# A two-layer decoder trunk: forget gates projected ahead of queries, norms by pairs and by log and exp, conditioning products ahead of the recurrence, weights two blocks ahead

## The chip, the cores and the metric

The kernel runs on one core of one Trainium2 chip. The metric is the device time of one execution in microseconds (us). The time before is 1189.71 us, the median of 3 runs (1188.65 to 1191.13). The profile is of one further execution.

## The reference, cut to what matters

A sequence of 256 tokens with 1024 features passes six sub-layers: feed-forward, recurrence (HGRN2), feed-forward, feed-forward, gated MLP, feed-forward. Each sub-layer has a norm before and behind it, and a shift, a scale and a gate that come from one vector `c`.

```python
mod = (silu(c) @ ada_w[i] + ada_b[i])            # shift, scale, gate of three sub-layers
def sublayer(x, fn, pre_g, post_g, shift, scale, gate, res_w):
    h = rms_norm(x, pre_g) * (1.0 + scale) + shift
    return x + res_w * gate * rms_norm(fn(h), post_g)

def hgrn2_mix(h, w_in, w_out, out_norm, lb):
    q, f, i, g = split(h @ w_in)                 # 1024 columns each, 8 heads of 128
    q = silu(q)
    log_f = logaddexp(log(lb), log1p(-lb) + log_sigmoid(f))
    k = (1.0 - lb) * sigmoid(-f)
    ...                                          # per head, chunks of 64: S_t = diag(f_t) S_{t-1} + k_t i_t^T
    o = rms_norm(o, out_norm) * silu(g)          # o_t = S_t^T q_t, norm per head
    return o @ w_out
```

## The kernel before, in words

**Weights.** Every weight block is 1 MB and comes in two halves (`cast`, `sub`): SyncE issues a load into one of four `raw` buffers (L121), ScalarE rounds the half to the high part (L122), VectorE subtracts to make the low part (L132). Products take three passes (high by high, high by low, low by high). The blocks stand in one list in the order of their use; `next_block` makes blocks until more than `ahead` are ready. High and low parts take buffers of a pool of 14. `proj`, `feat` and `tok` project with these blocks.

**Conditioning products.** The vector from `c` is made by 144 products on VectorE (`ada`, L192), each with a load of 512 KB into one of three buffers (after the first sub-layer has begun), issued by the same SyncE queue, in program order with the weights. `pace(upto, blocks)` spreads them: `wblock` makes both halves of a block, adds `rate` to a credit, and makes one product for each whole credit. `gate_tile` and `pre_cols` call for those that are still missing where they are used (products up to 24s+24 for the gate of sub-layer s, up to 24s+16 for its shift and scale).

**The recurrence sub-layer** (`hgrn`): two half projections of the output gate `g` and the values `v` stand in the sub-layer's entry (`boundary`, `proj`). Then come `feat` for the queries of heads 0 to 3, `feat` for their forget gates with `gate_f` (absolute value, exp and log on ScalarE, running sums on VectorE), and the recurrence `attn(0)`, stepped by `zip_steps` against `feat` for the queries and gates of heads 4 to 7 and `tok` for the other values. `attn` has a diagonal product (L718), then seven levels of 64, 32, ... 1 rows: VectorE prepares an operand (L741, L746), ScalarE takes the exponential (L80), VectorE multiplies (L752), TensorE makes the product (L758), VectorE merges it (L729); between two levels TensorE runs a part of the projections. Last come the outputs (L793). `attn(1)` runs beside `norm` (of the first four heads), `tok` for the rest of `g`, and `outs` (transposes L836, `split` L844 and L845, output products). Behind it stand the norm of the other heads (`stats`, `turn`) and the `boundary` to the next sub-layer.

**Order.** In `open()` to `close()` regions the instructions run as written; elsewhere a scheduler orders each engine's queue by program order and readiness. ScalarE, VectorE and TensorE take their queues in order, so an instruction that waits holds all behind it.

Of the kernel before, what the change touches and what calls it, by code (L numbers as in the profile page):

```python
# [18 lines left out]
P = 128  # L19
# [6 lines left out]
EPS = 1e-6  # L26
# [7 lines left out]
class Body:  # L34
# [272 lines left out]
    def boundary(self, y, G, mm, cols, table, plan=(4, 2, 0, 0)):  # L307
# [40 lines left out]
        gated(1, 0, yg1)  # L348
        self.alloc_h()
# [32 lines left out]
        dve = self.h_low(1, 1, self.h_full(1, pa1, cols))  # L382
        self.halves(1)
# [101 lines left out]
    def ffn(self, f, hT, G_fn, pre_next, nxt, bg):  # L485
# [100 lines left out]
        if f == 0:  # L586
            self.pace(bg, 23)
        for u in range(len(pend), 11):
# [17 lines left out]
            if u == 8:  # L606
                G = G_fn()
        pre_next()
# [35 lines left out]
    def hgrn(self, hT, G_fn, pre_next, nxt, bg):  # L644
        nc, tc = self.nc, self.tc
        self.pace(bg, 8)
# [152 lines left out]
        def stats(hb, ops, sqrt):  # L799

            ss = self.tiny.tile([P, 8], F32, tag="ss8", name="ss8")
            r = self.tiny.tile([P, 8], F32, tag="r8", name="r8")
            og, sqs = self.t4(), []
            for u in range(2):
                sqs.append(self.t2().rearrange("p (i v) -> p i v", i=4))
                nc.scalar.activation(sqs[u], ops[u].rearrange("p t h v -> p (t h) v"), AF.Square)

            def gated(u):
                c0 = 2 * (2 * hb + u) * P
                nc.vector.tensor_mul(og[:, 512 * u:512 * u + 512].rearrange("p (t c) -> p t c", t=NT),  # L810
                                     ops[u].rearrange("p t h v -> p t (h v)"), gg[:, :, c0:c0 + 2 * P])

            for u in range(2):
                nc.vector.reduce_sum(ss[:, 4 * u:4 * u + 4], sqs[u], axis=mybir.AxisListType.X)
                if u == 0:
                    gated(0)
            nc.vector.tensor_scalar(ss, ss, 1.0 / P, EPS, op0=ALU.mult, op1=ALU.add)
            if sqrt:
                self.tact(ss, ss, AF.Sqrt)
                self.cast()  # L820
                gated(1)
                nc.vector.reciprocal(r, ss)
            else:
                gated(1)
                self.rsqrt(r, ss)
            return og, r

        def turn(hb, u, og, r):

            on = og[:, 512 * u:512 * u + 512].rearrange("p (i v) -> p i v", i=4)  # L830
            for i in range(4):
                nc.vector.tensor_scalar(on[:, i, :], on[:, i, :], r[:, 4 * u + i:4 * u + i + 1], None, op0=ALU.mult)
# [89 lines left out]
        def norm():  # L922
            with tc.high_priority(offset=400):
                state["norm"] = stats(0, ops[0], False)
            yield

        def outs():
            for u in range(2):
                split(0, u, turn(0, u, *state["norm"]))
# [8 lines left out]
        y = []  # L938
        zip_steps(attn(1, bank_a, ops[1]), [
# [4 lines left out]
        self.table("sqrt_and_others")  # L944
        self.ahead = 0
        fill = products(1)
        wos = [nb()]
        self.ahead = 1
        wos.append(nb())
        self.open()  # L950
        self.gate = state["ops"]
        for op in fill[:5]:
            op()
# [5 lines left out]
        for op in fill[6:]:  # L959
            op()  # L960
        for u in range(2):
            split(1, u, ps[u])
# [338 lines left out]
```

## Time and profile before

| what | us |
|---|---|
| median of 3 runs | 1189.71 |
| profiled execution | 1182.1 |
| its span, first to last instruction | 1180.3 |
| TensorE busy | 1141.9 |
| VectorE busy | 904.6 |
| ScalarE busy | 665.9 |

Busy times are unions over an engine's instructions. Matmuls are pipelined, so TensorE's busy time says only where it stood still; how fast it went is read from the distance between the starts of two matmuls and from the granted clock (PEclk).

### The profile page before, as it was taken

To read this page: it belongs to the slowest core of one execution; us is meant where nothing else is said; L and a number is where in the kernel's file an instruction comes from. 1 tells how busy PE (TensorE), PEld (TensorE's weight loads), DVE (VectorE), ACT (ScalarE), POOL (GpSimd) and SP (SyncE) were. 2 spreads that over 40 slices of the span, in tenths; PEclk is the share of its full clock that TensorE was granted. 3 is DMA by queue.
4 is the path that set the end of the run, shared out by engine and by line. 5 is a ranking of instruction groups with operands and counts; after the bars stand their busy time and mean duration, and the time that the engine had idled before them with its cause. 6 is when DMAs were issued, how large, how long until landed. Compare 5 with 4: busy or idle time off the path is not lost.

```text
span 1180.3 us, 17103 instructions
## 1 busy us (share of the span) xinstructions
PE 1141.9 (97%) x6518; PEld 997.0 (84%) x6518; DVE 904.6 (77%) x1379; ACT 665.9 (56%) x1046; POOL 6.8 (1%) x16
## 2 busy tenths in 40 slices
PE   7999999997988999999999999999999999999997
PEld 6999998896877788888888888888989988888886
DVE  6997866899878799886599887466878776865752
ACT  6554436667636865556566555564665367654541
POOL 0000000000000000000000000000000000000000
PEclk9999999997989999999999999999999999999999
DMA  9889986597224399887279988526777773777630
GB/s 355 308 315 339 315 297 213 189 345 269 86 76 160 112 355 354 321 310 233 99 275 345 339 307 276 188 81 207 264 272 248 259 260 108 244 239 226 218 126 36
DMA packets 79765, 282.31 MB, mean 239 GB/s; under 512 B 9874, under 2 KB 10562, under 8 KB 79683
## 3 DMA queue, kind: packets, MB, share of 16 engines
q1 hardware_dynamic: 78626, 278.05, 67.4%
q0 software_dynamic: 1056, 3.17, 0.8%
q8 instruction: 51, 0.84, 0.3%
q14 instruction: 32, 0.25, 0.1%
HBM read 280.11 MB, written 1.07 MB: 238 GB/s over the span
## 4 chain that ended last, share of the span: by engine, by line
PE 77%; DVE 9%; DMA 8%; ACT 4%; issue 2%; SPq 0%; DVEq 0%; ACTq 0%
PE ups L454 17%; PE ups L455 9%; PE y L164 8%; PE y L162 8%; PE y L163 8%; PE pps L429 7%; PE ups L574 4%; DVE w L132 3%; DMA ada<-in_ada 3%; DMA raw<-in_wgmu 2%; PE ups L460 2%; PE ups L462 2%; PE ups L461 2%; PE ab L758 2%; ACT w L122 2%
## 5 line engine op out<-in xcount | busy, mean ns | idle before, releaser
L132 DVE TENSOR_TENSOR w<-raw,w 128x1024 fp32r<-128x1024 f32 x376 | 453.2, 1221 | 87.0 <-ACT w L122 85.4
L122 ACT CAST w<-raw 128x1024 fp32r<-128x1024 f32 x376 | 387.6, 1049 | 158.0 <-DMA raw<-in_wffn 75.3
L454 PE MATMUL ups<-h,w 128*128 128x512 f32 x864 | 302.1, 393 | 0.0
L455 PE MATMUL ups<-h,w 128*128 128x256 f32 x864 | 242.0, 280 | 0.0
L192 DVE CUSTOM_DVE_ANT_0 ada<-ada,cond 128x1024 f32<-128x1024 f32 x144 | 173.9, 1219 | 33.0 <-DMA ada<-in_ada 33.0
L454 PEld LDWEIGHTS ups<-h,w 128*128 128x128 f32 x864 | 161.7, 187 | 36.5
L162 PE MATMUL y<-w,t 128*128 128x512 f32 x448 | 178.6, 399 | 1.6 <-ACT t L167 1.6
L164 PE MATMUL y<-w,t 128*128 128x512 f32 x448 | 177.3, 396 | 0.4 <-DVE t L168 0.4
L163 PE MATMUL y<-w,t 128*128 128x512 f32 x448 | 177.3, 396 | 0.0
L455 PEld LDWEIGHTS ups<-h,w 128*128 128x128 f32 x864 | 163.3, 189 | 1.0
L460 PE MATMUL ups<-h,w 128*128 128x256 f32 x416 | 118.4, 285 | 0.0
L462 PE MATMUL ups<-h,w 128*128 128x256 f32 x416 | 117.7, 283 | 0.0
L461 PE MATMUL ups<-h,w 128*128 128x256 f32 x416 | 117.6, 283 | 0.0
L429 PE MATMUL pps<-w,h 128*128 128x512 f32 x480 | 113.9, 393 | 0.8 <-DVE be L242 0.8
L429 PEld LDWEIGHTS pps<-w,h 128*128 128x128 f32 x480 | 89.0, 188 | 19.4 <-DVE h L291 1.2
L162 PEld LDWEIGHTS y<-w,t 128*128 128x128 f32 x448 | 84.3, 188 | 21.5 <-ACT t L167 2.5
L164 PEld LDWEIGHTS y<-w,t 128*128 128x128 f32 x448 | 84.2, 188 | 21.4 <-DVE t L168 1.2
L163 PEld LDWEIGHTS y<-w,t 128*128 128x128 f32 x448 | 84.3, 188 | 18.2 <-DVE w L132 0.3
L460 PEld LDWEIGHTS ups<-h,w 128*128 128x128 f32 x416 | 79.7, 192 | 1.1 <-issue 0.2
L461 PEld LDWEIGHTS ups<-h,w 128*128 128x128 f32 x416 | 79.7, 192 | 0.8 <-issue 0.2
L462 PEld LDWEIGHTS ups<-h,w 128*128 128x128 f32 x416 | 79.7, 192 | 0.0
L80 ACT ACTIVATE t<-t 128x256 f32<-128x256 f32 (+2 forms) x70 | 36.1, 522 | 51.3 <-DVE t L507 39.0
(198 smaller groups left out, 1321.3 us busy)
## 6 DMA issues: line engine op xcount, KB each, us to landing
raw<-in_wffn SPq DMA_DIRECT2D x264, 512.0 KB, 5.7
ada<-in_ada SPq DMA_DIRECT2D x144, 512.0 KB, 6.7
raw<-in_wgmu SPq DMA_DIRECT2D x48, 512.0 KB, 5.8
raw<-in_whg SPq DMA_DIRECT2D x40, 512.0 KB, 5.9
raw<-in_wgmv SPq DMA_DIRECT2D x24, 512.0 KB, 4.6
G<-gflat POOLq DMA_DIRECT2D x6, 512.0 KB, 5.9
t<-in_gbin SPq DMA_DIRECT2D x6, 256.0 KB, 5.4
x<-in_x SPq DMA_DIRECT2D x2, 512.0 KB, 4.2
```

Of the source, the lines that this page charges most:

```text
L122: self.after(self.nc.scalar.copy(hi[:, sl], raw), self.hold[0])
L132: self.after(self.nc.vector.tensor_sub(lo[:, sl], raw, hi[:, sl]), self.hold[1])
L162: self.paced(mm(ps, l[0], r[0], start=start, stop=False))
L163: mm(ps, l[0], r[1], start=False, stop=False)
L164: mm(ps, l[1], r[0], start=False, stop=stop)
L192: self.after(nc.vector.tensor_tensor_reduce(t, t, self.cond, 1.0, 0.0, ALU.mult, ALU.add, self.mod[i // 24][:, i % 24:i % 24 + 1]), self.h ...
L429: lambda g=g, i=i, j=j, kc=kc, w=w: mm(res[g][t], h2[:, i, t, kc, :], w, start=kc + i + j == 0, stop=i == 1 and kc == KC - 1)))
L454: self.paced(mm(ps, u[0], self.h2[:, :, :, kc, :], start=kc == 0, stop=False))
L455: self.last = mm(ps[:, 1, :], u[1], self.h2[:, 0, :, kc, :], start=False, stop=kc == KC - 1)
L460: self.paced(mm(o, u[0], h[0], start=start, stop=False))
L461: mm(o, u[0], h[1], start=False, stop=False)
L462: self.last = mm(o, u[1], h[0], start=False, stop=stop)
```

## The change

- `hgrn`: the forget gates of heads 0 to 3 are projected and worked on first, then their queries; the tables of ScalarE are loaded for that order (two loads more). The weight list is reordered to match.
- `norm` (first four heads): log and exp on ScalarE and one correction step of four small instructions on VectorE take the place of an inverse root by three steps on VectorE; the scaling by it moves from `turn` into `norm`.
- The norm of the other four heads runs by pairs of heads: mean, root, gate, scale and transpose of the first pair, then those of the second, whose scaling is on ScalarE. The filling output products are laid around it in another way.
- `wblock`: the credit grows by half a rate after each half, so that a product can stand between two halves.
- `pace` and `boundary`: 46 products are made ahead of the recurrence sub-layer where 40 were; two of them in the boundary. The remaining 18 up to number 64 are spread over 11 blocks (before, 24 over 8).
- `ahead` is 2 in the second recurrence where it was 1; the boundary behind the recurrence makes one half more at its start and one more in its last part.

```diff
     def wblock(self):
-        self.halves(2)
-        self.credit += self.rate
-        while self.credit >= 1:
-            self.credit -= 1
-            self.ada(min(self.ada_next + 1, self.limit))
+        for _ in range(2):
+            self.halves(1)
+            self.credit += self.rate / 2
+            while self.credit >= 1:
+                self.credit -= 1
+                self.ada(min(self.ada_next + 1, self.limit))
...
     def boundary(..., plan=(4, 2, 0, 0), ada=(0, 0)):
         gated(1, 0, yg1)
+        self.ada(self.ada_next + ada[0])
         self.alloc_h()
...
         dve = self.h_low(1, 1, self.h_full(1, pa1, cols))
+        self.ada(self.ada_next + ada[1])
         self.halves(1)
...
     def ffn(...):
-            self.pace(bg, 23)
+            self.pace(36, 19)
...
             if u == 8:
                 G = G_fn()
+                if f == 0:
+                    self.pace(bg, 10)
...
     def hgrn(...):
-        self.pace(bg, 8)
+        self.pace(bg, 11)
...
-        def stats(hb, ops, sqrt):
...
+        def squares(ops):
+            sq = self.t2().rearrange("p (i v) -> p i v", i=4)
+            nc.scalar.activation(sq, ops.rearrange("p t h v -> p (t h) v"), AF.Square)
+            return sq
+        def mean(sq):
+            v = self.tiny.tile([P, 4], F32, tag="ss4", name="ss4")
+            nc.vector.reduce_sum(v, sq, axis=mybir.AxisListType.X)
+            nc.vector.tensor_scalar(v, v, 1.0 / P, EPS, op0=ALU.mult, op1=ALU.add)
+            return v
+        def gated(hb, u, ops):
+            og, c0 = self.t2(), 2 * (2 * hb + u) * P
+            nc.vector.tensor_mul(...)
+        def scale(og, r, scalar=False):
+            for i in range(4):
+                if scalar:
+                    nc.scalar.activation(og[:, i, :], og[:, i, :], AF.Copy, scale=r[:, i:i + 1])
+                else:
+                    nc.vector.tensor_scalar(og[:, i, :], og[:, i, :], r[:, i:i + 1], None, op0=ALU.mult)
...
-        run(feat(lambda pr, ps: self.tact(qs(0, pr), ps, AF.Silu)))
-        kn.append(self.wtile(F32))
         self.table("natural_log_exp_and_others")
         self.hg_cols()
+        kn.append(self.wtile(F32))
         run(feat(lambda pr, ps: gate_f(0, pr, ps)))
+        self.table("silu_and_others")
+        run(feat(lambda pr, ps: self.tact(qs(0, pr), ps, AF.Silu)))
+        self.table("natural_log_exp_and_others")
...
         def norm():
             with tc.high_priority(offset=400):
-                state["norm"] = stats(0, ops[0], False)
+                sqs = [squares(o) for o in ops[0]]
+                ...
+                self.tact(r, v, AF.Ln)
+                self.act_exp(r, r, scale=-0.5)
+                state["norm"] = [gated(0, u, ops[0][u]) for u in range(2)]
+                ...                      # q = r*r*v, r = r*(1.5 - 0.5*q): four instructions
+                for u in range(2):
+                    scale(state["norm"][u], r[:, 4 * u:4 * u + 4])
...
+        self.ahead = 2
         zip_steps(attn(1, bank_a, ops[1]), [...])
...
-        for op in fill[:5]:
+        for op in fill[:6]:
             op()
-        og, r = stats(1, ops[1], True)
-        ps = [turn(1, 0, og, r)]
-        fill[5]()
-        ps.append(turn(1, 1, og, r))
+        sqs = [squares(o) for o in ops[1]]
+        ps = []
+        for u in range(2):
+            v = mean(sqs[u])
+            r = self.tiny.tile([P, 4], F32, tag="r4", name="r4")
+            self.tact(v, v, AF.Sqrt)
+            og = gated(1, u, ops[1][u])
+            nc.vector.reciprocal(r, v)
+            if u:
+                split(1, 0, ps[0])
+            scale(og, r, u == 1)
+            if u:
+                fill[7]()
+            ps.append(turn(og))
+            if u == 0:
+                fill[6]()
+                self.cast()
+        split(1, 1, ps[1])
...
-        plans = {0: (0, 2, 1, 3), 1: (3, 1, 1, 0)}
-        bgs = {"ffn0": 40, "hg": 64, "ffn1": 92, "ffn2": 120, "gm": 138, "ffn3": 144}
+        plans = {0: (0, 2, 1, 3), 1: (4, 1, 1, 1)}
+        bgs = {"ffn0": 44, "hg": 64, "ffn1": 92, "ffn2": 120, "gm": 138, "ffn3": 144}
...
-    for c0 in (3072, 2048, 0, 1024, 512, 1536, 2560, 3584):
+    for c0 in (3072, 2048, 1024, 0, 512, 1536, 2560, 3584):
```

What the queues then hold is shown at three places. The first is VectorE at the start of the first recurrence, before: the diagonal product's mask (L719), weight halves (L132), conditioning products (L192, whose second row only reads the sum), then the operand of level 64 (L741) and its multiply (L752). Names carry buffer numbers here.

```order
L719 TENSOR_TENSOR t4_2945<-ab_2952,ident_113 128x512
L132 TENSOR_TENSOR w_2883<-raw_2884,w_2882 128x1024
L132 TENSOR_TENSOR w_2883<-raw_2888,w_2882 128x1024
L192 ISA ada_2892,mod2_108<-ada_2892,cond_112 128x1024
L192 ISA mod2_108 128x1
L192 ISA ada_2895,mod2_108<-ada_2895,cond_112 128x1024
L192 ISA mod2_108 128x1
L192 ISA ada_2898,mod2_108<-ada_2898,cond_112 128x1024
L192 ISA mod2_108 128x1
L741 TENSOR_TENSOR t4_3002<-w_2398,w_2557 128x8x64
L132 TENSOR_TENSOR w_2902<-raw_2903,w_2901 128x1024
L752 TENSOR_TENSOR t4_3002<-t4_3002,w_2398 128x8x64
```

The same place of the change, where these lines are L725, L132, L194, L747 and L758:

```order
L725 TENSOR_TENSOR t4_2932<-ab_2933,ident_113 128x512
L747 TENSOR_TENSOR t4_2989<-w_2416,w_2443 128x8x64
L132 TENSOR_TENSOR w_2892<-raw_2900,w_2891 128x1024
L725 TENSOR_TENSOR t4_2932<-ab_2939,ident_113 128x512
L758 TENSOR_TENSOR t4_2989<-t4_2989,w_2416 128x8x64
L774 TENSOR_TENSOR t4_3003<-w_2416,w_2443 128x4x64
L777 TENSOR_TENSOR t4_3003<-t4_3003,w_2416 128x4x64
L747 TENSOR_TENSOR t4_3050<-w_2416,w_2443 128x16x32
L752 TENSOR_TENSOR t4_3050<-w_2416 128x16x32
L194 ISA ada_3136,mod2_108<-ada_3136,cond_112 128x1024
L194 ISA mod2_108 128x1
```

Three products stood between the mask and the first level; now none does, and the operands of the next level (`t4_3050`) come at once behind it. Of the weight halves one stands there where there were three.

The second place is TensorE between the two recurrences, before: the second half of the outputs of the first four heads (L793, L791), then level 64 of the second recurrence (`t4_3339`) and the state product behind it (L778).

```order
L793 MATMUL ab_3276<-w_2393,t4_2945 128x128 x2
L791 MATMUL ab_3276<-w_2393,t2_3036 128x128
L793 MATMUL ab_3276<-w_2393,t4_2945 128x128
L791 MATMUL ab_3276<-w_2393,t2_3036 128x128
L793 MATMUL ab_3276<-w_2393,t4_2945 128x128
L758 MATMUL ab_3344<-t4_3339 128x64 x8
L778 MATMUL ab_3368<-t4_3353 128x128 x4
L162 MATMUL tps_3375<-w_3203,h2_2170 128x512
```

And of the change, with L764 for the levels and L799, L797 for the outputs; the first row is the last level of the first recurrence:

```order
L764 MATMUL ab_3255<-t4_3250,w_2443 128x64 x8
L764 MATMUL ab_3336<-t4_3331 128x64 x8
L799 MATMUL ab_3265<-w_2411,t4_2932 128x128 x2
L797 MATMUL ab_3265<-w_2411,t2_3023 128x128
L799 MATMUL ab_3265<-w_2411,t4_2932 128x128
L797 MATMUL ab_3265<-w_2411,t2_3023 128x128
L799 MATMUL ab_3265<-w_2411,t4_2932 128x128
L799 MATMUL ab_3272<-w_2411,t4_2932 128x128 x2
```

Level 64 of the second recurrence (`t4_3331`) now stands ahead of the outputs and of all that the norm does with them.

The third place is VectorE behind the second recurrence, before: the last merge (L729), weight halves, sums of squares (L814), gates (L810), mean (L817), inverse (L822) and scaling (L832).

```order
L729 COPY_PREDICATED t_3294<-lmask,ab 128x512
L132 TENSOR_TENSOR w<-raw,w 128x1024 x4
L814 TENSOR_REDUCE ss_3668<-t_3671 128x4
L810 TENSOR_TENSOR t_3670<-ab,w 128x512
L132 TENSOR_TENSOR w<-raw,w 128x1024
L814 TENSOR_REDUCE ss_3668<-t_3673 128x4
L132 TENSOR_TENSOR w<-raw,w 128x1024
L817 TENSOR_SCALAR ss_3668<-ss_3668 128x8
L810 TENSOR_TENSOR t_3670<-ab,w 128x512
L822 RECIPROCAL r_3669<-ss_3668 128x8
L832 TENSOR_SCALAR t_3670<-t_3670,r_3669 128x128 x8
```

And of the change, with L812, L813, L819, L975 and L828 for these steps:

```order
L812 TENSOR_REDUCE ss_3655<-t_3651 128x4
L813 TENSOR_SCALAR ss_3655<-ss_3655 128x4
L819 TENSOR_TENSOR t_3660<-ab,w 128x512
L975 RECIPROCAL r_3658<-ss_3655 128x4
L828 TENSOR_SCALAR t_3660<-t_3660,r_3658 128x128 x4
L812 TENSOR_REDUCE ss_3680<-t_3653 128x4
L813 TENSOR_SCALAR ss_3680<-ss_3680 128x4
L819 TENSOR_TENSOR t_3685<-ab,w 128x512
L975 RECIPROCAL r_3683<-ss_3680 128x4
```

The two weight halves that stood inside the norm's chain are gone from it, and the first pair's scaling no longer waits for the second pair's sums.

More of the change, by code (lines that the diff above doesn't have):

```diff
@@ L305, in open, with boundary @@
         self.region.__enter__()
-    def boundary(self, y, G, mm, cols, table, plan=(4, 2, 0, 0)):
+    def boundary(self, y, G, mm, cols, table, plan=(4, 2, 0, 0), ada=(0, 0)):
         nc = self.nc
@@ L797, in attn @@
             yield
-        def stats(hb, ops, sqrt):
[L801 to L826, printed above, removed]
@@ L828, in turn @@
-        def turn(hb, u, og, r):
-            on = og[:, 512 * u:512 * u + 512].rearrange("p (i v) -> p i v", i=4)
-            for i in range(4):
-                nc.vector.tensor_scalar(on[:, i, :], on[:, i, :], r[:, 4 * u + i:4 * u + i + 1], None, op0=ALU.mult)
+        def squares(ops):
[7 more added lines that the diff above has]
+            return v
@@ L833, in turn @@
+        def turn(on):
             ps = self.acc.tile([P, 512], F32, tag="acc", name="ots")
@@ L923, in norm @@
             with tc.high_priority(offset=400):
-                state["norm"] = stats(0, ops[0], False)
+                sqs = [squares(o) for o in ops[0]]
+                v, r, q = [self.tiny.tile([P, 8], F32, tag=n, name=n) for n in ("ss8", "r8", "q8")]
+                for u in range(2):
+                    nc.vector.reduce_sum(v[:, 4 * u:4 * u + 4], sqs[u], axis=mybir.AxisListType.X)
+                nc.vector.tensor_scalar(v, v, 1.0 / P, EPS, op0=ALU.mult, op1=ALU.add)
+                self.tact(r, v, AF.Ln)
+                self.act_exp(r, r, scale=-0.5)
+                state["norm"] = [gated(0, u, ops[0][u]) for u in range(2)]
+                nc.vector.tensor_mul(q, r, r)
+                nc.vector.tensor_mul(q, q, v)
+                nc.vector.tensor_scalar(q, q, -0.5, 1.5, op0=ALU.mult, op1=ALU.add)
+                nc.vector.tensor_mul(r, r, q)
+                for u in range(2):
+                    scale(state["norm"][u], r[:, 4 * u:4 * u + 4])
             yield
@@ L928, in outs @@
             for u in range(2):
-                split(0, u, turn(0, u, *state["norm"]))
+                split(0, u, turn(state["norm"][u]))
             yield
@@ L944, in hgrn @@
         self.table("sqrt_and_others")
+        fill = products(1)
         self.ahead = 0
[L946 to L949, printed above, removed]
+        wos = [nb(), nb()]
         self.open()
         self.gate = state["ops"]
-        for op in fill[:5]:
+        for op in fill[:6]:
             op()
-        og, r = stats(1, ops[1], True)
-        ps = [turn(1, 0, og, r)]
-        fill[5]()
-        ps.append(turn(1, 1, og, r))
+        sqs = [squares(o) for o in ops[1]]
+        ps = []
+        for u in range(2):
+            v = mean(sqs[u])
[13 more added lines that the diff above has]
+        split(1, 1, ps[1])
         self.sub()
[L959 to L962, printed above, removed]
         nxt(y, G, self.out_last(y, oTs[2:], wos))
@@ L1187, in nxt @@
                         self.open()
-                    self.boundary(y, G, mm, st["cols"], tables[subs[s + 1][0]], plans.get(s, (4, 2, 0, 0)))
+                    self.boundary(y, G, mm, st["cols"], tables[subs[s + 1][0]], plans.get(s, (4, 2, 0, 0)),
+                                  (1, 1) if s == 0 else (0, 0))
                     self.hT = self.h2[:, 0], self.h2[:, 1]
```

3 lines of the change are left out of this document (added).

## The prediction, made before the change was timed

> **What bounds the kernel now.** I read the page's head first, then a table of stages, then the starts of single matmuls, and only then the waits.
>
> ```profile
> span 1180.3 us, 17103 instructions
> PE 1141.9 (97%) x6518; PEld 997.0 (84%) x6518; DVE 904.6 (77%) x1379; ACT 665.9 (56%) x1046; POOL 6.8 (1%) x16
> ```
>
> TensorE (PE) is busy 97% of the span, so the kernel as a whole is bound by it, and a change that leaves the number of matmuls alone can win only where TensorE stands still or runs slowly. The table of stages (busy time of PE, its weight loads, DVE, ACT, POOL; granted clock; DMA share and GB/s) says where:
>
> ```profile
> core 0: us, PE busy (x) PEld busy (x) DVE busy (x) ACT busy (x) POOL busy (x), PEclk, DMA share, GB/s
> 160.00:200.00 40.00, 40.00 (x245) 35.60 (x244) 25.71 (x34) 19.68 (x25) 0.56 (x1) 1.00 0.74 253
> 250.00:300.00 50.00, 38.05 (x250) 35.69 (x248) 48.32 (x78) 35.74 (x63) 0.00 (x0) 0.82 0.77 274
> 320.00:340.00 20.00, 16.34 (x98) 14.99 (x98) 16.21 (x34) 8.36 (x19) 0.55 (x1) 0.83 0.37 131
> 340.00:366.00 26.00, 26.00 (x168) 23.41 (x167) 17.92 (x33) 12.95 (x15) 0.00 (x0) 1.00 0.12 39
> 366.00:382.00 16.00, 11.82 (x60) 9.70 (x60) 14.34 (x24) 9.16 (x13) 0.00 (x0) 0.89 0.65 218
> 420.00:440.00 20.00, 20.00 (x119) 17.68 (x118) 19.92 (x32) 13.02 (x22) 0.00 (x0) 1.00 0.98 371
> ```
>
> Three stretches lose time: 12.0 us idle in 250 to 300, 3.7 in 320 to 340, 4.2 in 366 to 382. All three lie in the recurrence sub-layer, which the change rearranges. The clock is low there too, and what that costs shows in the starts of four matmuls of one kind:
>
> ```profile
> 254.72 0.28 PE L462 MATMUL fps<-h,w 128*128 128x256 f32 x1
> 254.84 0.28 PE L460 MATMUL fps<-h,w 128*128 128x256 f32 x1
> 278.10 0.41 PE L460 MATMUL fps<-h,w 128*128 128x256 f32 x1
> 278.32 0.41 PE L461 MATMUL fps<-h,w 128*128 128x256 f32 x1
> ```
>
> At full clock the next one starts 0.12 us later, behind a long wait 0.22. By the mean clock the three stretches lose 50 x 0.18 = 9.0, 20 x 0.17 = 3.4 and 16 x 0.11 = 1.8 us more (part of it while PE is idle anyway). So some 20 us idle, and up to 14 of slow running, are there to be won; outside there is little.
>
> The waits of PE between 225 and 395 us (total, times, longest):
>
> ```profile
> PE ots L836 <- DVE t L832: 4.2, 1, 4.2
> PE fps L462 <- DVE w L132: 4.0, 3, 2.9
> PE ab L758 <- DVE rs_sh L88: 3.2, 1, 3.2
> PE ab L758 <- ACT t L80: 3.0, 1, 3.0
> PE ab L758 <- DVE t L752: 2.3, 1, 2.3
> ```
>
> Read in order of time: weights late (L132: 4.0), the first levels late (L80, L752: 5.3), level 64 of the second recurrence behind the norm's arithmetic (L88: 3.2), the last transposes behind the scaling (L832: 4.2). Why the weights are late stands in SyncE's own waits from 225 to 290 us and in two steps of the chain of waits:
>
> ```profile
> SPq L57 <- DVE mod L192: 49.3, 18, 11.8
> 267.60 7.10 DMA raw<-in_whg
> 275.52 7.04 DMA raw<-in_whg
> ```
>
> The one load queue stood 49.3 of 65 us behind buffers of conditioning products that VectorE had not worked off, three between two blocks; weights were issued late, and each then took 7 us. VectorE was 48.32 of 50 us busy: it is the bound of that stretch.
>
> **The change, part by part.** The durations of VectorE and ScalarE, per group from 225 to 395 us (count, busy us, mean ns), and two rows in which operations of 512 columns start 0.60 us apart back to back:
>
> ```profile
> L132 DVE TENSOR_TENSOR w<-raw,w 128x1024 fp32r<-128x1024 f32 x37 | 44.5, 1221 | 6.3 <-ACT w L122 5.8
> L192 DVE CUSTOM_DVE_ANT_0 ada<-ada,cond 128x1024 f32<-128x1024 f32 x24 | 28.5, 1219 | 2.6 <-DMA ada<-in_ada 2.6
> L704 DVE TENSOR_TENSOR_SCAN w<-rmask,w 128x256 f32<-128x256 f32 x8 | 5.0, 670 | 0.0
> L702 DVE SCALAR_TENSOR_TENSOR w<-w,loglb,L 128x256 f32<-128x256 f32 x8 | 3.5, 475 | 0.0
> L729 DVE COPY_PREDICATED t<-lmask,ab 128x512 f32<-128x512 int32 x14 | 12.5, 892 | 8.3 <-PE ab L758 8.3
> L122 ACT CAST w<-raw 128x1024 fp32r<-128x1024 f32 x36 | 36.6, 1044 | 22.5 <-DMA raw<-in_whg 14.4 <-PE fps L461 5.2 <-DMA raw<-in_wffn 2.9
> L80 ACT ACTIVATE L<-L 128x512 f32<-128x512 f32 x16 | 10.0, 622 | 0.1
> L74 ACT ACT_TABLE_LOAD x5 | 6.4, 1283 | 0.1
> 290.82 0.68 DVE L741 TENSOR_TENSOR t<-w 128x512 f32<-128x512 f32 x1
> 291.42 0.68 DVE L746 TENSOR_TENSOR t<-w 128x512 f32<-128x512 f32 x1
> ```
>
> A weight half costs VectorE 44.5/37 = 1.20 us, a conditioning product 28.5/24 = 1.19, one `gate_f` 2 x 0.60 + 2 x 0.63 + 4 x 0.44 = 4.2 (its L707 taken as L702).
>
> *To the first recurrence.* This stretch starts at the first `feat` matmul:
>
> ```profile
> 229.79 0.28 PE L460 MATMUL fps<-h,w 128*128 128x256 f32 x1
> 221.65 1.22 DVE L132 TENSOR_TENSOR w<-raw,w 128x1024 fp32r<-128x1024 f32 x1
> ```
>
> TensorE has 312 `feat` matmuls ahead of the first diagonal product, ready at the earliest at 229.8 + 312 x 0.12 = 267.2. VectorE has, from 221.65 on, 16 weight halves (19.2), 15 products (17.9), two `gate_f` (8.4) and about 1 us of small ones: 46.5, done at 268.2. Both come out even. The queue holds two weight blocks more ahead of the first multiply of a level than before, and three products fewer between. With one product between two halves in place of three, the load queue waits one product's time; DMA moves 27 pieces of 0.52 MB in 45 us, 315 GB/s, under the 371 shown above. So the waits for weights go; if it reaches no more than the 253 to 274 GB/s of two other rows, 27 pieces take 52 to 56 us, and the first rival below holds. ScalarE has 16 casts (16.6), 6 table loads (7.7), two `gate_f` (four operations at 0.62 and seven shorter ones, about 6 each, an estimate) and some 7 us of copies and silu: 43 of 46 us. It fits, narrowly.
>
> A rule of the Trainium skill speaks against the change. In the row above five table loads take 1283 ns each with 0.1 us idle ahead of all five. It (ScalarE: Activation LUTs, What ACT_TABLE_LOAD costs) gives the same 1283 ns, and about 1380 ns of drain on top, for every switch. By the row the two added loads cost ScalarE 2.6 us. By the page they cost 5.3, and the sum below would be smaller by 2.7. The trace shows no such idle time, so the sum goes by the row.
>
> *Through the first recurrence.* From 268.2 VectorE is the bound: to the multiply of level 2 (h = 2) it has 5 halves, 2 products, two `gate_f`, 22 operations at 0.60, four merges and two short ones: 6.0 + 2.4 + 8.4 + 13.2 + 3.5 = 33.5, hence near 302. Before, a part of the chain gave level 2, and a row of the timeline level 32 of the second recurrence, at
>
> ```profile
> 319.08 1.75 PE ab L758 x16
> 341.66 0.44 PE L758 MATMUL ab<-t 128*128 128x64 f32 x3
> ```
>
> *Into the second.* VectorE's queue from level 2 to that multiply of level 32: 4 halves (4.8), 2 products (2.4), 3 merges (2.7), 12 operations of 0.60 (7.2), 8 scalings (1.7 for eight, below) and 1.2 of small ones: 20.0, so level 32 starts near 322.3, 19.4 us earlier than before. TensorE has 14 us of work between the two marks (three levels at 1.75, two parts of 12 matmuls at 0.23, 32 short ones at about 0.11), is there near 316.6 and waits 5.7 us: the norm, with its scaling, now stands ahead of level 32 on VectorE. That wait takes the place of the one for L88. Behind it the clock is low again: some 20 matmuls at 0.22 for 0.12, minus 2.0 us (from nothing, if the levels are waited for anyway, to 3.4, the loss by clock in 320 to 340). The norm's log and exp on 8 columns do not show in the trace; between nothing and the 0.62 of 512 columns each, I take 0.2, and they lie beside VectorE's halves.
>
> *Waits that I did not see.* VectorE was 3.4% idle even where it was the bound (48.32 of 50). Over the 100 us walked that is minus 3.4; at least 0, at most 9, if waits grow as large as the halves' own idle time ahead of them before (6.3 in L132's row) and the products' (2.6).
>
> *Behind the second recurrence.*
>
> ```profile
> 371.44 0.69 DVE L814 TENSOR_REDUCE ss<-t 128x4 f32<-128x512 f32 x1
> 377.25 1.66 DVE L832 TENSOR_SCALAR t<-t,r 128x128 f32<-128x128 f32 x8
> 371.75 0.39 PE L164 MATMUL y<-w 128*128 128x512 f32 x1
> 371.98 0.39 PE L162 MATMUL y<-w 128*128 128x512 f32 x1
> 385.22 0.60 ACT L235 ACTIVATE junka<-y 128x512 bf16<-128x512 f32 x1 [0.75 <-PE y L164]
> ```
>
> Before, 5.8 us lie between the first sum and the scaling; two weight halves and the other pair stood between. Now one pair takes sum 0.6, mean and root 0.4, gate 0.6, inverse 0.2, scaling 0.8: 2.6, against 18 filling products of 0.23 (4.1 us). The wait of 4.2 goes, and with it 1.8 us of low clock less what the second pair's scaling on ScalarE is late (0.3): plus 5.7. It could be only 4 if that pair waits 2 us. The boundary starts with one half more: ScalarE ended its three casts 0.75 us ahead of the square at 385.22, and now has four casts with 1.4 us less output product to hide them, so the chain to the next transposes starts later: minus 1.2 (0 to 2.5).
>
> *Elsewhere.* Four products move into the first feed-forward and two into the boundary behind it (7.1 us of VectorE, 8.5 of DMA at 371 GB/s). From 160 to 200 TensorE was busy throughout while VectorE had 14.3 of 40 us free and DMA a quarter: 0, or minus 2 if a late load holds the half behind it. A product between two halves in the other stages: 0 plus or minus 2, since each is made anyway.
>
> **Sum.** 19.4 - 2.0 - 3.4 + 5.7 - 1.2 = 18.5 us off the profiled execution (1180.3 of span, 1182.1 in all): 1163.6. The median of the runs lies 7.6 above that execution; I take the same 18.5 off it: **1171.2 us**.
>
> **The rivals.**
> - *The feed still binds.* If VectorE slips by more than 3 us before 268, the weights for the last gates come behind their matmuls again, with low clock behind. For: both engines fill their 46 us to 93% or more. Against: the load queue's 49.3 us of waits lose their cause. Gain 3 to 12, about 1182; 0.17.
> - *The waits go almost wholly*, as both engines find work in the gaps: gain 22 to 30, about 1164; 0.09.
> - *The table loads cost ScalarE double*, a drain per switch: 2.6 us more in a queue with 3 us to spare; level 64 comes that much later: 1173.8. Row L74 speaks against it; 0.04. (The rule of the Trainium skill above, ScalarE: Activation LUTs, says so.)
> - *It does not do what it says*: the sub-layer ends earlier, but the next feed-forward, whose feed is full (VectorE 19.92 of 20, DMA 0.98 in 420 to 440), then waits for weights. Against: DMA lay at 0.12 from 340 to 366, so there is room to load earlier. 1189.7; 0.05.
> - *Slower.* In the two full feed-forwards and the gated MLP 74 products are now laid between halves; each delays a second half by 1.19 us. From 16 of them uncovered (18.5/1.19) the gain is gone; with half of all, 44 us are lost: 1215. Against: TensorE is 20.00 of 20 busy at clock 1.00 there, though products stood ahead of the next block's halves before. 0.05.
>
> **How the numbers follow.** The forecast (gain 12 to 22, 1168 to 1178) has 0.60. The range takes it in whole, most of the first rival and the near part of the second: 1163 to 1184. Faster by over 0.2% (2.4 us, about what a measurement can tell from no change): 0.60 + 0.17 + 0.09 + 0.04 = 0.90; within 0.05; slower 0.05.
>
> **What would show it.** Right: SyncE's waits for products between 225 and 290 far under 49 us; no wait for L132 or L122 before 267; level 2 of the first recurrence near 302; one wait of about 6 us ahead of level 32 of the second, released by VectorE; none above 1 us at the last transposes. Wrong: PE idle on weights from 250 to 280; VectorE's sum between those marks longer than 33 and 20 us; new waits of PE in 420 to 460 or in the gated MLP.

## The result, and the profile after

| | before | after |
|---|---|---|
| median of 4 runs, us | 1189.18 (1183.73 to 1191.13) | 1174.91 (1173.04 to 1177.66) |
| profiled execution, us | 1182.1 | 1173.04 |
| its span, us | 1180.3 | 1171.2 |

The ratio of the runs is 0.9889 (95% interval 0.9849 to 0.9929): 13 us faster, between 8 and 18. The two profiled executions lie only 9.1 us apart by their spans, since the one of before was faster than any of the four runs; a second profile of before is among the experiments.

The head of the page of after, and TensorE's waits from 225 to 395 us (total, times, longest), then two of SyncE's from 225 to 290:

```profile
span 1171.2 us, 17067 instructions
PE 1135.3 (97%) x6518; PEld 992.9 (85%) x6518; DVE 902.0 (77%) x1369; ACT 669.1 (57%) x1055; POOL 6.8 (1%) x16
PE ab L764 <- DVE t L758: 12.2, 4, 6.2
PE npa L271 <- DVE be L244: 5.9, 1, 5.9
SPq L57 <- DVE w L132: 30.3, 12, 9.1
SPq L57 <- DVE mod L194: 12.0, 7, 3.1
```

Of the waits of before, those for weights (4.0 and 2.0), for the root (3.2) and for the last scaling (4.2) are gone; SyncE stands 12.0 us behind products where it stood 49.3. It now stands 30.3 us behind weight halves that have not yet freed a `raw` buffer (2.3 before): the loads run ahead of VectorE and no longer behind it. TensorE waits for no weights in the whole stretch. Four waits for VectorE's operands are left (12.2), and a wait of 5.9 us for a row statistic is new. The matmuls that the prediction named, from the timeline of after (start, duration, engine, line, operation; in brackets the idle time ahead and what ended it):

```profile
231.16 0.28 PE L464 MATMUL fps<-h,w 128*128 128x256 f32 x1
308.76 0.44 PE L764 MATMUL ab<-t 128*128 128x64 f32 x2 [2.14 <-DVE t L758]
329.61 0.69 PE L764 MATMUL ab<-t 128*128 128x64 f32 x2 [6.19 <-DVE t L758]
383.59 0.69 PE L271 MATMUL npa<-ident,xn 128*128 128x128 f32 x2 [5.90 <-DVE be L244]
```

These are the first projection matmul of the stretch, level 2 of the first recurrence, level 32 of the second, and the first transpose in the boundary behind. The table of stages for them (columns as in the prediction):

```profile
250.00:300.00 50.00, 46.12 (x341) 44.28 (x340) 45.45 (x73) 40.95 (x68) 0.00 (x0) 0.93 0.58 200
320.00:340.00 20.00, 13.81 (x69) 11.99 (x68) 17.56 (x36) 7.43 (x10) 0.00 (x0) 0.83 0.38 128
376.00:392.00 16.00, 9.65 (x40) 7.47 (x39) 11.98 (x25) 12.46 (x30) 0.00 (x0) 0.79 0.44 159
```

From 250 to 300 TensorE is now idle 3.9 us (before, 12.0) at a clock of 0.93 (0.82). From 376 to 392, in the boundary, it is idle 6.4 at a clock of 0.79.

To lay idle and slow time together, I take for every matmul the distance from its start to the next start, less the median distance of its kind (0.23 us for 512 columns, 0.12 for 256, 0.11 for the shorter ones). Summed up, this is the time that TensorE lost:

| TensorE's lost time, us | before | before, second profile | after |
|---|---|---|---|
| up to the first projection matmul of the recurrence | 15.8 | 17.3 | 17.2 |
| from there to level 32 of the second recurrence | 33.6 | 34.5 | 20.2 |
| to the last transposes | 1.9 | 1.9 | 4.4 |
| at the last transposes | 6.2 | 8.3 | 0.8 |
| boundary behind the recurrence | 2.0 | 1.9 | 8.8 |
| all behind it | 15.7 | 18.2 | 14.9 |
| sum | 75.3 | 82.1 | 66.3 |

How the kinds are cut moves the rows themselves by several us, but their differences between kernels by 1 to 2 us. The second row can be had without kinds: from the first projection matmul to level 32 there are 111.9 us before and 98.4 after.

So 13.4 us come from the first long stretch and 5.4 from the last transposes; 2.5 and 6.8 go back. The difference of the sums, 9.0, is nearly that of the spans (9.1).

Nearly all of the 13.4 lies ahead of level 64 of the first recurrence. It started 56.8 us behind the first projection matmul before (at 286.6) and 44.1 after (at 275.3); from there to level 32 of the second there are 55.1 and 54.4 us. The diagonal product started 37.0 us behind that matmul before and 37.4 after, so the place is between it and level 64. There VectorE was busy 18.4 of 19.8 us before; six conditioning products stood ahead of the operand of level 64, which it began at 282.56. ScalarE was as late, since a cast ahead of the exponential waited 4.92 us for its load:

```profile
282.59 1.05 ACT L122 CAST w<-raw 128x1024 fp32r<-128x1024 f32 x1 [4.92 <-DMA raw<-in_whg]
```

### The profile page after: what moved, and what is told of

Its sections match the earlier page's. It is cut to its first block, busy times and chain, and to the rows that moved or that the text cites. A ratio compares the mean times of both kernels' runs of the same rounds, so it can differ in the third digit from the quotient of the medians.

```text
span 1171.2 us, 17067 instructions
## 1 busy us (share of the span) xinstructions
PE 1135.3 (97%) x6518; PEld 992.9 (85%) x6518; DVE 902.0 (77%) x1369; ACT 669.1 (57%) x1055; POOL 6.8 (1%) x16
## 4 chain that ended last, share of the span: by engine, by line
PE 86%; DVE 6%; DMA 4%; ACT 2%; issue 2%; DVEq 0%; SPq 0%; ACTq 0%
PE ups L458 17%; PE y L164 9%; PE y L166 9%; PE y L165 9%; PE ups L459 9%; PE pps L433 8%; PE ups L578 4%; PE ups L464 3%; PE ups L466 3%; PE ups L465 3%; PE ab L764 2%; DVE w L132 2%; DMA raw<-in_wgmu 1%; DMA ada<-in_ada 1%; PE pps L164 1%
## 5 line engine op out<-in xcount | busy, mean ns | idle before, releaser
L132 DVE TENSOR_TENSOR w<-raw,w 128x1024 fp32r<-128x1024 f32 x376 | 452.4, 1220 | 89.3 <-ACT w L122 88.4
L194 DVE CUSTOM_DVE_ANT_0 ada<-ada,cond 128x1024 f32<-128x1024 f32 x144 | 174.5, 1218 | 25.3 <-DMA ada<-in_ada 25.1
```

The lines of the kernel that those rows point to most:

```text
L132: self.after(self.nc.vector.tensor_sub(lo[:, sl], raw, hi[:, sl]), self.hold[1])
L194: self.after(nc.vector.tensor_tensor_reduce(t, t, self.cond, 1.0, 0.0, ALU.mult, ALU.add, self.mod[i // 24][:, i % 24:i % 24 + 1]), self.h ...
```

## The experiments

Theory: the fewer products among the recurrence's weights free the load queue, and the boundary's loss is a cast that waits for its weights ahead of a row statistic. Rivals: the new order of gates and queries carries the gain; the boundary's weights are late in any order. All kernels compute the whole reference. Before had medians of 1187.5, 1186.1 and 1187.4 us in the three groups of runs (kernels 1 to 4, 5 to 8, 9 to 12); each ratio is to the before of its own group, so kernels of different groups are better compared by their ratios. `ahead` and the norm by pairs were not tried alone.

**1. Boundary plan.** The casts ahead of and between the two row statistics of the first block are counted by the plan.

```diff
-        plans = {0: (0, 2, 1, 3), 1: (4, 1, 1, 1)}
+        plans = {0: (0, 2, 1, 3), 1: (3, 0, 0, 4)}
```

> The kernel after, but the four casts that the boundary behind the recurrence makes ahead of its first row statistic and the one between the two statistics become three and none; the four left over come behind the last transposes' statistics (plan 3, 0, 0, 4). Theory: in the profile of the kernel after, the fourth cast waits 3.16 us for its weights (issued at 370.13, landed at 374.12), and the squares of y stand behind it on ScalarE, so TensorE stands 6.06 us at 377.30 and runs some 1.8 us slowly behind. Then that stall falls under 1.5 us and the kernel is 6 to 7 us faster than the kernel after (about 1168). Rival 1, the feed is late whatever its order: the stall goes from 377 but comes back as a wait for weights between 384 and 400; within 2 us of the kernel after (1173 to 1177). Rival 2, the row statistics themselves are the chain: the stall keeps at least 4 us; within 2 us.

Measured: 1172.7 us, ratio 0.9871 (0.9843 to 0.9900). What the edit was aimed at shows first in ScalarE's timeline of after:

```profile
368.05 2.94 ACT L122 CAST w<-raw 128x1024 fp32r<-128x1024 f32 x3
374.14 1.05 ACT L122 CAST w<-raw 128x1024 fp32r<-128x1024 f32 x1 [3.16 <-DMA raw<-in_wffn]
375.10 0.59 ACT L237 ACTIVATE junka<-y 128x512 bf16<-128x512 f32 x1
377.10 1.05 ACT L122 CAST w<-raw 128x1024 fp32r<-128x1024 f32 x1 [1.32 <-DMA raw<-in_wffn]
378.05 0.59 ACT L237 ACTIVATE junka<-y 128x512 bf16<-128x512 f32 x1
```

The fourth cast stands 3.16 us for its weights, the cast between the statistics another 1.32, and each square of `y` stands behind one. In the experiment the wait of the boundary's first transpose fell from 5.9 to 0.5 us, as the theory has it; but with four casts in a row further on, the next transposes waited 1.6 us, so that the boundary's loss fell from 8.8 to 4.7 only. And up to the boundary its order is that of after, word for word, yet level 32 stood 102.7 us behind the first projection matmul (98.4 in after):

```profile
230.05 0.28 PE L464 MATMUL fps<-h,w 128*128 128x256 f32 x1
332.74 0.47 PE L764 MATMUL ab<-t 128*128 128x64 f32 x1 [6.20 <-DVE t L758]
```

So one profile of this order tells that distance only to about 4 us, and the median moved 2 us instead of 6 to 7: the theory was right on the place, and the size stayed open.

**2 and 3. The layout of the products undone, and alone.** Kernel 2 is after with the old layout (its half credit stays), kernel 3 is before with the new one (half credit included). The edit of kernel 2:

```diff
-            self.pace(36, 19)
+            self.pace(bg, 23)
...
-                if f == 0:
-                    self.pace(bg, 10)
...
-        self.pace(bg, 11)
+        self.pace(bg, 8)
...
-        bgs = {"ffn0": 44, ...}
+        bgs = {"ffn0": 40, ...}
...
-                                  (1, 1) if s == 0 else (0, 0))
+                                  (0, 0))
```

> The kernel after with the conditioning products laid out as before (40 ahead of the recurrence sub-layer in place of 46, 24 inside it at the old rate), all else as after. Theory: the products between blocks hold up the load queue; SyncE's waits for products between 225 and 290 us return from 12 to over 30 us, the projection matmuls wait for weights again (3 to 8 us idle ahead of the first recurrence), and the kernel is 4 to 10 us slower than after (1179 to 1185). Rival, the new order of gates and queries carries the gain by itself: within 2 us of after.

> The kernel before with the new layout of the conditioning products alone (46 ahead, a half's credit at a time, the old order of queries and gates, the old norms). Theory, the load queue held by products is the larger cause: SyncE's waits for products between 225 and 290 us fall from 49 to under 25 us, TensorE's 4.0 us of waits for weights go, and 4 to 8 us are gained on the kernel before (1181 to 1185); the gates still come last, so the first level's waits (3.0 and 2.3 us) stay or grow. Rival, the order carries it: less than 2 us gained.

Measured: kernel 2 1178.3 (0.9913, 0.9886 to 0.9939); kernel 3 1172.1 (0.9871, 0.9842 to 0.9900), more than expected. Some of SyncE's and TensorE's waits in kernel 2, then in kernel 3:

```profile
SPq L57 <- DVE mod L194: 47.3, 20, 11.2
PE fps L464 <- ACT w L122: 3.9, 3, 2.8
PE fps L466 <- DVE w L132: 3.4, 5, 1.3
```

```profile
SPq L57 <- DVE mod L193: 11.9, 7, 3.0
PE ots L841 <- DVE t L837: 5.1, 1, 5.1
PE ab L763 <- DVE rs_sh L88: 3.2, 1, 3.2
PE fps L465 <- DVE w L132: 0.8, 1, 0.8
```

With the old number of products the queue's waits are back, and so are the projections' waits for weights (7.3 us); with the new number and the half credit alone both nearly go. The first levels' waits, which were expected to stay or grow, are 3.5 and 2.0 us in kernel 3 (2.3 and 3.0 before). Level 64 of the first recurrence, 56.8 us behind the first projection matmul before and 44.1 after, is 49.1 behind it in kernel 2 and 45.3 in kernel 3. The new layout alone is worth 15.4 us, everything else (with the half credit) 9.2, both together about 14: the parts do not add up.

**4. Queries first.** After, with the old order of the projections.

```diff
-        run(feat(lambda pr, ps: gate_f(0, pr, ps)))
-        self.table("silu_and_others")
         run(feat(lambda pr, ps: self.tact(qs(0, pr), ps, AF.Silu)))
         self.table("natural_log_exp_and_others")
+        self.hg_cols()
+        run(feat(lambda pr, ps: gate_f(0, pr, ps)))
...
-    for c0 in (3072, 2048, 1024, 0, 512, 1536, 2560, 3584):
+    for c0 in (3072, 2048, 0, 1024, 512, 1536, 2560, 3584):
```

> The kernel after with the queries projected ahead of the forget gates again, all else as after. Theory: two gate computations (8.4 us on VectorE, some 12 on ScalarE) then stand between the last of the 312 projection matmuls and the first levels; TensorE waits 4 to 8 us more there, level 2 of the first recurrence starts that much later, 1179 to 1184. Rival, the products moved away carry the gain and VectorE's sum up to level 2 is the same in either order: within 2 us of after, with the same VectorE sum.

Measured: 1170.1 (0.9851, 0.9821 to 0.9882), the opposite of the theory: 4.8 us less than the median of after (4.5 by the ratios), and its runs (1168.8 to 1171.8) lie below all of after's. From the first projection matmul to level 32 there are 95.9 us:

```profile
229.91 0.28 PE L464 MATMUL fps<-h,w 128*128 128x256 f32 x1
325.77 0.47 PE L764 MATMUL ab<-t 128*128 128x64 f32 x1 [5.72 <-DVE t L758]
```

**5. Queries first, and a better boundary.** Kernel 4 with plan (3, 0, 1, 3).

> The kernel with queries projected first (the last run above, median 1170.1) and, behind the recurrence, the boundary's casts laid out 3, 0, 1, 3: none between the two row statistics, one where its weights have landed, three ahead of the second block's statistics. Theory: the cast that waits for its weights ahead of the row statistics costs 5.7 us of wait and 1.3 of low clock at the boundary; with it moved, and one fewer ahead of the second block than in the plan 3, 0, 0, 4 (which brought back 1.8 us there), 4.5 to 6.5 us are gained on 1170.1: about 1164 to 1166. Rival, the row statistics' chain is the limit or the weights are late anyway: within 2 us of 1170.

Measured: 1165.3 (0.9838, 0.9808 to 0.9869), 4.8 us under kernel 4, with no overlap of the runs. ScalarE in the boundary, and the transpose that waited:

```profile
365.54 2.94 ACT L122 CAST w<-raw 128x1024 fp32r<-128x1024 f32 x3
368.37 0.59 ACT L237 ACTIVATE junka<-y 128x512 bf16<-128x512 f32 x1
371.67 1.05 ACT L122 CAST w<-raw 128x1024 fp32r<-128x1024 f32 x1
375.81 0.66 PE L271 MATMUL npa<-ident,xn 128*128 128x128 f32 x4 [0.64 <-DVE be L244]
```

The square follows the third cast, the fourth finds its weights there, and 5.5 us of waiting in kernel 4 (5.9 in after) become 0.64. Both rivals on the boundary fall: neither the statistics nor the weights' arrival bound it, but the casts' place in ScalarE's queue.

**6. Four more products ahead.** Kernel 5 with 50 products in place of 46.

```diff
-            self.pace(36, 19)
+            self.pace(38, 19)
...
-        bgs = {"ffn0": 44, ...}
+        bgs = {"ffn0": 48, ...}
```

> The run above (queries first, plan 3, 0, 1, 3) with 50 products in place of 46 ahead of the recurrence sub-layer: four more in the first feed-forward, four fewer among the recurrence's weights. Theory, VectorE's queue is the bound up to level 2 of the first recurrence: each product taken out is worth its 1.2 us as far as it stood ahead of that level, so level 2 starts 2 to 5 us earlier and 2 to 5 us are gained on that run; the first feed-forward takes them without a new wait, since TensorE was never idle from 160 to 200 us. Rival 1, the chain of levels between VectorE, ScalarE and TensorE is the bound by now: nothing gained, more idle time of VectorE. Rival 2, the first feed-forward's feed is full: new waits of TensorE for weights before 229 us, 1 to 4 us lost.

Measured: 1162.2 (0.9808, 0.9780 to 0.9836); the runs (1160.6 to 1165.5) overlap those of kernel 5 (1164.1 to 1168.1). Level 2 stands 75.2 us behind the first projection matmul (76.0 in kernel 5), not 2 to 5 us earlier, and level 32 stands 96.2 us behind it in both. So the profile bears out no gain ahead of level 32, and the medians' 3.1 us cannot be told from the spread of the runs; a wait of 1.2 us is new in the boundary ahead of the recurrence:

```profile
PE npa L271 <- DVE be L244: 1.2, 1, 1.2
```

**7. Scaling in turn.** Kernel 5, with the eight scalings at their use in `outs`.

```diff
-                for u in range(2):
-                    scale(state["norm"][u], r[:, 4 * u:4 * u + 4])
...
+                scale(state["norm"][u], state["r"][:, 4 * u:4 * u + 4])
                 split(0, u, turn(state["norm"][u]))
```

> The run with queries first and plan 3, 0, 1, 3, and the eight scalings of the first norm (1.65 us on VectorE) moved from ahead of level 32 of the second recurrence to where they are used. Theory, level 32 waits for VectorE's queue and nothing else: that wait falls from about 6 to about 4.2 us, the transposes are not later for it, 1.5 to 2 us are gained on that run. Rival, VectorE has no room behind either: the 1.65 us come back as a wait at the transposes or at a later level, within 1 us of that run.

Measured: 1163.6 (0.9819, 0.9791 to 0.9847), 1.7 us under kernel 5, though the runs of the two overlap (1162.0 to 1166.5, 1164.1 to 1168.1). The wait ahead of level 32 fell as expected, by 1.56, level 32 stands 95.2 us behind the first projection matmul (96.2), and no wait of TensorE behind it is new up to 395 us:

```profile
230.16 0.28 PE L464 MATMUL fps<-h,w 128*128 128x256 f32 x1
325.40 0.69 PE L764 MATMUL ab<-t 128*128 128x64 f32 x2 [4.15 <-DVE t L758]
```

**8. Before, once more.**

> The kernel before, unchanged, for a second profile. Its runs lie between 1183 and 1191 us and the profiled one was the fastest (1182.1). If the spread is made where TensorE waits for weights in the recurrence sub-layer (225 to 300 us), a profile of a slower run shows level 2 of the first recurrence later than 319.1 by about what the run is longer; if it is made in the clock at the start or in later stages, level 2 stands within 1.5 us of it.

Measured: 1189.1 us, 7.0 more than the first profile. Level 2 stands 2.5 us later, of which 1.5 were lost ahead of the recurrence. Most of the rest lies at the last transposes (2.1) and behind the boundary (2.5), so the spread has no one place: neither expectation holds, the second is nearer.

**9. Both last edits together.** Kernel 7 with 50 products.

> The two last edits together: queries first, plan 3, 0, 1, 3, the eight scalings where they are used, 50 products ahead of the recurrence sub-layer. Theory: the scaling's 1.7 us are gained in either layout; the four products gain little, since level 32 of the second recurrence stood 296.2 us behind... the same 96.2 us behind the first projection matmul with 46 and with 50, and a new wait of 1.3 us for them stood at 203. So 1161 to 1163.5, within 2 us of the run with the scaling alone (1163.6). Rival, the 3.1 us between the two medians (1165.3 and 1162.2) are a gain of the products: then 1159 to 1161.

Measured: 1162.3 (0.9796, 0.9771 to 0.9821), within the theory's range (the 296.2 in it is a slip for 96.2). It is the lowest ratio of all, but its median is that of kernel 6 (1162.2): next to kernel 6 the scaling's 1.7 us do not show, so neither small edit is told from the spread by its time. VectorE's share tells more; the stage from 250 to 300 in kernel 7, then in kernel 9 (the third number is VectorE's busy time):

```profile
250.00:300.00 50.00, 45.59 (x333) 43.83 (x333) 48.20 (x79) 42.71 (x76) 0.00 (x0) 0.93 0.62 214
250.00:300.00 50.00, 46.62 (x356) 44.79 (x355) 44.79 (x74) 42.67 (x78) 0.52 (x1) 0.97 0.51 175
```

VectorE has 3.4 us less to do there. Level 2 starts 75.3 us behind the first projection matmul (76.5 in kernel 7), but level 32 starts 95.5 us behind it against 95.2.

**10. Gates first again.** After with plan (3, 0, 1, 3) and the scaling in turn, so that only the order differs from kernel 7.

> The kernel after (gates projected first) with plan 3, 0, 1, 3 and the eight scalings where they are used: against the run with queries first and the same two edits (1163.6) only the order of the projection differs. Theory: projected first, the gates cost 3 to 6 us by level 32 of the second recurrence (98.4 and 102.7 us behind the first projection matmul in two profiles with gates first, 95.9 and 96.2 with queries first), so 1166 to 1170, and VectorE stands idle 4 us or more between level 64 and level 1 of the first recurrence. Rival, the difference of the medians with the order of after (1174.9 and 1170.1) is the spread of the runs: within 2 us of 1163.6.

Measured: 1170.8 (0.9858, 0.9830 to 0.9886); its runs (1167.9 to 1172.7) do not overlap those of kernel 7 (1162.0 to 1166.5); the medians lie 7.2 us apart, by the ratios 4.6. From 230.23 to level 32 there are again 102.7 us. VectorE's waits between level 64 and level 1 of the first recurrence, kernel 10 (42.7 us long) and then kernel 7 (35.5 us):

```profile
DVE t L735 <- PE ab L764: 2.6, 1, 2.6
DVE w L132 <- ACT w L122: 2.3, 1, 2.3
DVE t L725 <- PE ab L724: 1.8, 1, 1.8
DVE w L708 <- ACT L L80: 1.2, 1, 1.2
DVE t L758 <- ACT t L80: 0.7, 1, 0.7
```

```profile
DVE t L735 <- PE ab L764: 1.8, 1, 1.8
DVE ada L194 <- DMA ada<-in_ada: 0.5, 1, 0.5
DVE w L697 <- ACT L L80: 0.3, 1, 0.3
```

8.6 against 2.6 us: 6.0 of the 7.2 us by which the stretch is longer are waits of VectorE, nearly all on the other two engines in turn. Kernels 1 and 10 keep the order of after up to level 2, yet reach level 32 4 us later than it, so the size of the loss is uncertain by about that much.

**11 and 12. The norm's arithmetic, and the half credit.** Kernel 7, in 11 with the inverse root by shift and Newton steps on VectorE, in 12 with the credit per whole block.

```diff
-                self.tact(r, v, AF.Ln)
-                self.act_exp(r, r, scale=-0.5)
...
+                self.rsqrt(r, v)
```

> The run with queries first, plan 3, 0, 1, 3 and the scaling in turn, but the first norm's inverse root by the shift and three Newton steps on VectorE, as before, in place of log and exp on ScalarE. Theory: the norm's own way matters by its VectorE time alone (some ten short operations of 0.16 us for five, less the waits on ScalarE's queue between them): the wait ahead of level 32 of the second recurrence (4.3 us) becomes 4.5 to 5.5, 0 to 1.5 us lost. Rival, log and exp wait behind casts on ScalarE and are the slower way: 1 to 2 us gained.

> The run with queries first, plan 3, 0, 1, 3 and the scaling in turn, with the products credited per whole weight block, as before, in place of per half. Theory: with 46 products ahead there are fewer between the recurrence's weights, and it is their number, not their place, that held up the load queue (with the old number and the new credit SyncE still waited 47.3 us for them): SyncE's waits for products stay under 20 us and the time within 2 us of 1163.6. Rival, one product between two halves in place of two or three in a row is what freed the queue: waits over 25 us, 3 us or more lost.

Kernel 11: 1163.7 (0.9818, 0.9783 to 0.9852), the wait ahead of level 32 within 0.25 us of kernel 7: log and exp gain nothing that shows. Kernel 12: 1170.0 (0.9859, 0.9826 to 0.9891), 6.4 us over the median of kernel 7 (4.7 by the ratios) although the queue's waits stayed low. SyncE's wait for products, and TensorE's waits from 940 to 980 us, in the gated MLP, where kernel 7 has none:

```profile
SPq L57 <- DVE mod L193: 13.3, 7, 4.1
PE y L163 <- ACT t L168: 2.9, 2, 2.2
```

Level 32 stands 99.3 us behind the first projection matmul (95.2 in kernel 7). Between level 64 and level 1 of the first recurrence VectorE waits 7.3 us (2.6 in kernel 7): 3.0 for ScalarE, 2.5 for the load of a product. But these places do not show that the half credit is the cause. The profiled execution of kernel 11, which has the half credit and the order of kernel 7 up to level 1, took 1170.2 us where its other three runs took 1163.5 to 1163.7. It has level 32 at 98.5 and a wait of 2.2 us in the gated MLP as well. So whole credits are most likely slower, since every run of kernel 12 (1167.6 to 1173.0) is slower than every run of kernel 7, and the queue is freed by the products' number; where the half credit saves its time is open.

## Why the prediction was right, and where it was not

The forecast was 18.5 us off the median; 14.3 came, inside the forecast's main case and the range. By the first two profiles it was 9.0, by the second profile of before 15.8. So part of the hit is luck: the walk was made on the first profile of before, and against that one its terms missed by 9.5 us in sum, the boundary with 5.6 and level 32 with 2.6 above all. That the median still came within 4 us of the forecast is owed to the runs of before, whose median lies 7.1 us above the execution that was profiled; in after it lies 1.9 above.

- **Load queue and projections** (312 matmuls without a wait for weights): right. 231.16 + 312 x 0.12 = 268.6, where the diagonal starts. But the gain is not in them: before, the diagonal started as soon behind the first of them (with 294 matmuls ahead of it), and TensorE had waited 0.7 us for weights by then. Its other 5.3 us of waits for weights came behind the diagonal, and so did the late load and the products that held level 64. The reason given for the freed queue was wrong: "one product between two halves in place of three" did not free the queue. With half credits and the old number it waited 47.3 us, with whole credits and the new number 13.3.
- **Level 32, 19.4 less 3.4 for waits not seen** = 16.0: measured 13.4; level 2 came at 308.76, not near 302. The walk took VectorE for the bound and added up its queue, and the work in it was right: 53.5 us by the sum, 53.9 measured. But the engines wait for one another in turn. VectorE's waits in after, 268.5 to 329.7 us:

```profile
DVE t L725 <- PE ab L724: 1.8, 1, 1.8
DVE ada L194 <- DMA ada<-in_ada: 1.5, 1, 1.5
DVE w L708 <- ACT L L80: 1.2, 1, 1.2
DVE w L132 <- ACT w L122: 0.9, 1, 0.9
DVE t L735 <- PE ab L764: 0.9, 1, 0.9
DVE t L758 <- ACT t L80: 0.7, 1, 0.7
```

  With 0.3 more for one square these are 7.3 us in place of 3.4. Before had 8.1 us of them between the diagonal and level 32; the prediction took its 3.4% from 250 to 300 alone, where they are few. They seem to depend on the order, but single profiles spread widely: 7.3, 10.7 and 12.1 us with gates first (after, kernels 1 and 10), 2.5 to 7.7 with queries first and the new norms (kernels 4 to 7, 9, 11 and 12). The prediction took "gates first" for a part of the gain; it costs 5 to 7 us by the medians of kernels 4, 7 and 10, some 4.5 by the ratios. Kernel 9 shows the same failing from the other side: with 3.4 us less on VectorE level 32 came no earlier.
- **The wait ahead of level 32**: forecast 5.7, measured 6.19, by VectorE, and without the scaling in it it is 1.56 shorter (kernel 7). **Clock behind it**: forecast 2.0, measured 2.5. The granted clock was 0.50 from 329.6 to 335.0 and 0.88 from 335 to 337, some 5.9 us at half clock by these two numbers. The Trainium skill (TensorE: Matmul & The Clock Gate, Part 1) has some 3.4 us at half clock behind such a wait, which would be 1.7 lost, an estimate from that figure. The trace shows more.
- **Last transposes**: forecast plus 5.7, measured plus 5.4: right.
- **Boundary**: forecast minus 1.2 (0 to 2.5), measured minus 6.8. This is the step that failed. It counted "four casts with 1.4 us less output product" as casts in a row; it did not ask when the fourth one's weights land. There are four `raw` buffers, and VectorE's halves, which free them, came only behind the last pair's arithmetic:

```profile
368.85 4.62 DVE L132 TENSOR_TENSOR w<-raw,w 128x1024 fp32r<-128x1024 f32 x4
```

  The first of these frees a buffer at 370.07, the load is issued at 370.13, and its weights land at 374.12. Kernel 5 shows that place and price: with the casts moved, 4.8 us come back. So what the pairwise norm won at the transposes (5.4) was given back a few us later, in after.
- **Elsewhere**: forecast 0; 1.4 lost ahead of the recurrence (the second profile of before lost as much there) and 0.8 won behind it. Whether a product between two halves changes anything in other stages is not settled: kernel 12, without them, has the slower runs, but its wait in the gated MLP stands in kernel 11 too.
- **The rivals.** No wait of TensorE between 400 and 930 us is over 0.8, so the products between halves did no harm there. ScalarE's seven table loads from 225 to 395 us show no drain:

```profile
L74 ACT ACT_TABLE_LOAD x7 | 9.0, 1283 | 0.1
```

  The 1283 ns of the Trainium skill (ScalarE: Activation LUTs, What ACT_TABLE_LOAD costs) stand; of its further 1380 ns per switch there is no sign in this row, 0.1 us of idle time ahead of all seven.

In order of what the runs show: the layout of the products 15 us, of which the half credit is a part; norms, `ahead` and plan together some 2 more (1172.1 to 1170.1, within the noise), since the boundary ate what the transposes gained; gates first minus 5. With queries first, plan (3, 0, 1, 3), the scaling in turn and 50 products the kernel takes 1162.3 us, a further 12.6 under after.

## What to carry to other kernels

A walk along one engine's queue gives a floor, not a time, where three engines hand work to each other at every step: ask of each step which of the others it waits for, and price an order by these waits. Where a change brings work forward, ask of everything queued there when its input lands and which buffer that load waits for; ahead of a short critical chain, a cast that has to wait costs its whole wait. And test the parts of a change alone: here one part of it carried the gain, and another took a third of that back.

## What the runs showed that was not expected

An unchanged order of instructions had level 32 at 98.4 and at 102.7 us behind the same start, in two kernels that differ only later; with queries first, kernels 7 and 11 have one order up to level 1 and level 2 at 76.5 and 79.6. So in a stretch where engines take turns, one profile tells a distance only to 3 or 4 us. And the time that before lost on TensorE differed by 6.8 us between two of its executions (75.3 and 82.1), spread over several stages rather than at one wait.
